# Two-layer hybrid backbone on one core: filter unit ends spread over the next unit, spectra stored by GpSimd's queue, weights prepared with loads ahead, an early pool lower in SBUF

## The chip, the core and the metric

The kernel runs on one core of a Trainium2 chip. The metric is the device time of one execution in microseconds, lower is better. TensorE (PE) multiplies matrices, VectorE (DVE), ScalarE (ACT) and GpSimd (POOL) work on tiles, SyncE (SP) issues most of the transfers; each engine takes its instructions strictly in the order in which the program wrote them.

## The reference, cut to what matters

Layer 0 mixes a pooling branch with grouped-query attention, layer 1 mixes a Hyena branch (two long convolutions by FFT) with a Fourier branch. The change touches work that belongs to layer 1 but needs none of its inputs, and is done under the attention of layer 0: the Hyena filters with their spectra, and the weights in split form.

```python
def one_block(qblk):                       # layer 0, attention
    s = jnp.einsum('bqhgd,bkhd->bhgqk', qblk, k) * scale
    p = jax.nn.softmax(s, axis=-1).astype(v.dtype)
    return jnp.einsum('bhgqk,bkhd->bqhgd', p, v)
...
def hyena_filters(L, w1, b1, w2, b2, w3, freq):
    ...
    h = (hdn @ w3.astype(f32)).reshape(L, HY_ORDER, 2, HY_WIDTH)
    decay = jnp.exp(-t * jnp.abs(deltas))
    h = h * decay[:, None, None, :]
    h = h / (jnp.sum(jnp.abs(h), axis=(0, 2), keepdims=True) + EPS)
...
def fft_long_conv(z, kfull):
    zf = jnp.fft.rfft(z, n=2 * L, axis=1)
    kf = jnp.fft.rfft(kfull, n=2 * L, axis=0)
```

2048 tokens, 6 query heads of 128, 2304 keys (256 of context), and 12 filter units of 128 channels (6 groups of channels, 2 orders).

## The kernel before, in words

Five stages follow each other: the projections of layer 0 (to about 599 us), attention (to 1766), the output projection of layer 0 (to 2075), the projections of layer 1 (to 2808), and the convolutions' end, the Fourier branch and the output.

**Attention and what lies in it.** Attention walks 96 blocks (6 heads, 8 query tiles, 2 halves). The order within a block is a string `BLOCK[..]` of letters: `S` scores, `M` the maximum, `E` exponentials, `T` transposes, `V` products with the values, `D` and `N` the division. Two letters put other work between them. `F` (and `f` in every eighth pair of blocks) is a fill: it takes one step of the generator `filters`, and when that has ended, of `wout`. `p` takes one step of the generator `weights`. Strings 0 and 1 serve even and odd blocks until `filters` has ended, strings 2 and 3 after that. At that end `for _ in prep: pass` writes out what is left of `weights` in one go, before the next letter of the block; then its pool `aside` is closed.

**The filters.** 12 units of 8 groups. A group is a fill with the product `hacc` of the hidden features (`hd`) with `w3`, a DVE product `ht` with the decay (`dec`), a reduction `rd` of the absolute values, and a fill with the products `fa`, which ACT copies into the spectrum `fX`. At a unit's end the eight `rd` are reduced to `rs`, summed over the partitions on TensorE (`smacc`), and turned into a scale `sc_n` and the pair `sd`, from which the last `fa` comes: 18 fills for a unit. Then GpSimd transforms `fX` by an FFT of 46 instructions. `some()`, called in every fill, hands these to GpSimd's order: it lets `FFT_US` of the instructions' listed cost pass for each call. The finished spectrum (2 MB) is stored by SP, `FFT_LATE` fills after the last FFT instruction.

**The weights.** 23 items of the first kind (a block of the layer-1 input weights) and 32 of the second (output weights, multiplied by a gate). An item loads `wraw`, (second kind) multiplies it by `wgb` on GpSimd, casts it on ACT to the high half of `wodd`, subtracts on GpSimd to get the low half, and stores `wodd` through SP. An item of the second kind spreads over six `p`: load, multiply, nothing, cast, subtract, store. After the items come two products `fnp` with the DFT matrix.

Of the kernel before, what the change touches and what calls it, by code (L numbers as in the profile page):

```python
# [248 lines left out]
def tile_net(ctx, tc, i, k, out, keep=None):  # L249
# [233 lines left out]
    LASTE, LASTR, GATE2, FOLD1, HALF, SUM0, SUM1, ADDF, FEW, LASTW, IN_C, FFT_US, FFT_LATE, FILTER_X, HL, DR, DE, EW0, EW1, SPLIT, SUMMED, QSEL, CV0, CV1, CV2, CV3, COL, NW0, NW1, FIRST_Z, MORE, X0_SQ, X0_STEP, TRAIL, C_EARLY, A_TURN, A_SLOW, A_AHEAD, A_W, A_PACE, LAG0, FOLD, WAIT, AHEAD, LAG, APART, LOW, W_LOAD, W_HIGH, W_LOW, ADDED, SLOW = 0, 0.5, 5, 6, 1.5, 0.2, 1.5, 3, 9, 3.5, 25, 4.4, 4, 2, 3, 4, 4, 8.0, 2.5, 15, 0.5, 1, 14, 12, 8, 15, 5, 24, 0, 20.0, 8, [7, 7, 11, 11], (0, 0, 0, 0, 2, 2, 2, 2), 11, 1, 2.5, 0.25, 3.5, 4, 1.05, 7, 2, 6.0, 2.5, 5, 5, 2, 6, 6, 4, 8, 1.02  # L483
# [16 lines left out]
    with ExitStack() as st, tc.manual_schedule(engines=EVERY):  # L500
        sp = pool(st, "a_sb", 2)
# [5 lines left out]
        def pair(name):  # L507
            x2 = sp.tile([P, KD, 256], F32, tag="wmb", name=name)
# [47 lines left out]
        with ExitStack() as s2:  # L556
# [24 lines left out]
            hd2 = sp.tile([P, 4, 2, HD], F32, tag="sq", name="hd2", bufs=1).rearrange("p t h d -> p (t h d)")  # L581
# [208 lines left out]
        def heads(raw, ss, nt, tb, nm, dst, col0):  # L790
# [9 lines left out]
            else:  # L800
                rt = ropes[tb, nm]
                sq = sp.tile([P, 4, 2, HD], F32, tag="sq", name="sq", bufs=1)
# [30 lines left out]
        def modulation():  # L833
# [5 lines left out]
            def load(blk):  # L839
                n, c0 = (0, 2048 + 256 * blk) if blk < 4 else (1, 256 * (blk - 4))  # L840
                wms[blk] = sp.tile([P, KD, 256], F32, tag="wmb", name="wmb")
# [44 lines left out]
        def mixer():  # L886
# [3 lines left out]
            for m in range(2):  # L890
# [7 lines left out]
                uf = sp.tile([P, N2, P], F32, tag="wmb", name="uf")  # L898
                sy.dma_start(uf, src)
                sg = sp.tile([P, N2, P], F32, tag="wmb", name="psg")  # L900
                sy.dma_start(sg, sg0[m].rearrange("p (a b) -> p a b", a=N2))
                yield 0.0, 12.0
                for c in range(2):
                    c0 = 64 * c
                    us = sp.tile([P, 2, 32, 64], F32, tag="xt", name="us", bufs=1)
# [217 lines left out]
    def filters(st, psum, tag, after):  # L1123
# [8 lines left out]
        late, ops = [], []  # L1132
        got, room = {}, [0.0]

        def some():

            due[0] += 1
            room[0] = min(room[0] + FFT_US, FFT_US)
            while ops and room[0] > 0:
                us, op = ops.pop(0)  # L1140
                room[0] -= us
                if callable(op):
                    op()
                else:
                    late.append((due[0] + FFT_LATE, op))
            if late and late[0][0] <= due[0]:
                sy.dma_start(*late.pop(0)[1])

        due = [0]
# [9 lines left out]
        def fetch_w3(u):  # L1159
# [6 lines left out]
            skr = sp.tile([1, P], F32, tag="skr", name="skr", bufs=2)  # L1166
            sy.dma_start(skr, i["hy_skip"][0, o : o + 1, jl])
            got[u] = raw, skr

        def split_w3(u):  # L1170
            raw, skr = got[u]
# [3 lines left out]
            got[u] = w, skr  # L1175

        fetch(0, 0)
        fetch_w3(0)
        yield
# [3 lines left out]
        for u in range(2 * NCH):  # L1183
            j, o = u // 2, u % 2
            w3, skr = got.pop(u)
            rd = sp.tile([P, 8, P], F32, tag="rd", name="rd")
            X = sp.tile([P, 2, N2, P], F32, tag="X", name="fX", bufs=FILTER_X)
            for grp, (n, m) in enumerate(PAIRS):
                last = grp == 7
                if (u, grp) != (2 * NCH - 1, 7):  # L1190
                    fetch(u + grp // 7, (grp + 1) % 8)
                dec, hd = got.pop((u, grp))
                ht = sp.tile([P, 2, 2, P], F32, tag="ht", name="ht", bufs=2)
                acc = psum.tile([P, 2, 2, P], F32, tag=tag, name="hacc")
                for q in range(2):
                    for x in range(2):
                        w = w3[:, x, ::-1] if q else w3[:, x]
                        pe.matmul(acc[:, q], hd[:, q, :], w, start=x == 0, stop=x == 1)
                after(1, lambda: v.tensor_mul(ht, acc, dec.unsqueeze(2).to_broadcast([P, 2, 2, P])))
                yield  # L1200
                some()
                v.tensor_reduce(out=rd[:, grp, :], in_=ht.rearrange("p a d b -> p b (a d)"), axis=AX.X, op=ALU.add,
                                apply_absolute_value=True)
                if u + 1 < 2 * NCH and grp in (3, 6):
                    (fetch_w3 if grp == 3 else split_w3)(u + 1)
                if last:
                    rs = sp.tile([P, P], F32, tag="rs", name="rs")
                    v.tensor_reduce(out=rs, in_=rd.rearrange("p a b -> p b a"), axis=AX.X, op=ALU.add)
                    yield
                    sm = psum.tile([P, 512], F32, tag=tag, name="smacc")  # L1210
                    pe.matmul(sm[:, 0:1], rs, ones[:, 0:1], start=True, stop=True)
                    pe.matmul(sm[0:1, P : 2 * P], ones[:, 0:1], rs, start=True, stop=True)
                    sd = sp.tile([P, 2, 2, P], F32, tag="ht", name="sd", bufs=2)

                    def scaled():
                        idx = o * NCH + j
                        v.tensor_scalar(out=sc_n[:, idx : idx + 1], in0=sm[:, 0:1], scalar1=EPS, scalar2=None, op0=ALU.add)
                        rw = sp.tile([1, P], F32, tag="rw", name="rw")
                        v.scalar_tensor_tensor(out=rw, in0=sm[0:1, P : 2 * P], scalar=EPS, in1=skr, op0=ALU.add, op1=ALU.mult)
                        v.reciprocal(sc_n[:, idx : idx + 1], sc_n[:, idx : idx + 1])  # L1220
                        v.tensor_add(ht[0:1, 0, 0, :], ht[0:1, 0, 0, :], rw)
                        v.memset(ht[0:1, 0, 1, :], 0.0)
                        v.tensor_add(sd[:, 0], ht[:, :, 0], ht[:, :, 1])
                        v.tensor_sub(sd[:, 1], ht[:, :, 0], ht[:, :, 1])


                    after(2, scaled)
                    yield
                fa = psum.tile([P, 2, 2, P], F32, tag=tag, name="fa")
                for r in range(2):  # L1230
                    for q, b in enumerate((n, m)):
                        if last:
                            pe.matmul(fa[:, r, q], dft[:, b, r, :], sd[:, r, q], start=True, stop=True)
                        else:
                            pe.matmul(fa[:, r], dft[:, b, r, :], ht[:, q], start=q == 0, stop=q == 1)
# [1190 lines left out]
```

## Time and profile before

| what | us |
|---|---|
| median of 3 runs | 3177.69 (3174.78 to 3182.2) |
| the profiled execution | 3177.3 |
| its span | 3175.5 |
| TensorE busy in it | 2937.0 (92%) |
| attention stage, first to last | about 603 to 1766 |

The profiled execution is 0.4 us below the median and 1.8 us above its own span. Times inside the trace count from the start of the span. TensorE is busy nearly all the time, so what it waits for in a stage is what that stage could lose; its busy time also stretches where the granted clock is below 1.

### The profile page before, as it was taken

What the parts mean: (1) busy time and instruction counts of PE and PEld (TensorE: products, weight loads), DVE (VectorE), ACT (ScalarE), POOL (GpSimd) and SP (SyncE); (2) the same over time, 40 slices, a digit from 0 to 9 for tenths busy, and PEclk for the clock granted to TensorE, in tenths of its full rate; (3) what the DMA queues carried; (4) which work ended last, traced back from release to release, by engine and by line L of the source; (5) the groups of instructions that cost most, each with busy time, mean ns of one, the idle gap of its engine ahead of it and who ended that gap; (6) DMA issues with size and microseconds to landing.
All of it is one profiled execution on the core that took longest, in us unless ns stands there. A gap on an engine that the chain in (4) does not pass through costs nothing. (4 is left out here: it accounts for less than half of the span.)

```text
span 3175.5 us, 46860 instructions
## 1 busy us (share of the span) xinstructions
PE 2937.0 (92%) x16969; PEld 2520.1 (79%) x16969; DVE 2149.7 (68%) x3981; ACT 1323.7 (42%) x3048; POOL 1132.7 (36%) x1091
## 2 busy tenths in 40 slices
PE   7999999799999999999986999999989999988799
PEld 4898888688888888888875778777878777874587
DVE  4676327477777777777764343377879797978556
ACT  4444445365655555556554232322323222231223
POOL 3122122117877778788871344001010010100110
PEclk9999999899999999999998999999999999989899
DMA  6466335534443343333325577689899989976875
GB/s 219 147 206 206 107 135 172 168 100 129 128 134 115 112 148 105 112 118 112 104 77 214 183 268 252 242 268 292 275 307 277 289 275 302 278 235 184 218 205 175
DMA packets 346707, 602.74 MB, mean 190 GB/s; under 512 B 41894, under 2 KB 216168, under 8 KB 336490
## 3 DMA queue, kind: packets, MB, share of 16 engines
q1 hardware_dynamic: 321178, 516.37, 47.9%
q0 software_dynamic: 25152, 83.10, 11.1%
q8 instruction: 134, 2.20, 0.3%
q14 instruction: 99, 0.81, 0.1%
q10 hardware_dynamic: 144, 0.26, 0.0%
HBM read 376.80 MB, written 187.18 MB: 178 GB/s over the span
## 5 line engine op out<-in xcount | busy, mean ns | idle before, releaser
L312 DVE TENSOR_TENSOR pl<-pt,ph 128x512 fp32r<-128x512 f32 (+1 forms) x480 | 299.0, 633 | 171.8 <-ACT ph L309 165.0
L155 DVE TENSOR_TENSOR gB<-gB 128x256 f32<-128x256 f32 (+3 forms) x442 | 351.6, 845 | 47.6 <-ACT gB L1933 43.8
L1338 ACT ACTIVATE pb<-S,mx 128x512 f32<-128x512 f32 (+1 forms) x480 | 310.1, 657 | 161.2 <-DVE mx L1330 161.1
L315 PE MATMUL dacc<-dh,dw 128*128 128x512 f32 x768 | 311.4, 406 | 45.8 <-DMA dh<-h1T 44.5
L309 ACT CAST ph<-pt 128x512 fp32r<-128x512 f32 (+1 forms) x480 | 257.6, 556 | 220.0 <-PE pt L1349 218.8
L1327 DVE TENSOR_REDUCE mx<-S 128x1 f32<-128x512 f32 (+1 forms) x480 | 279.7, 629 | 54.4 <-PE S L317 40.5
L316 PE MATMUL dacc<-dh,dw 128*128 128x512 f32 x768 | 304.1, 396 | 0.0
L317 PE MATMUL dacc<-dh,dw 128*128 128x512 f32 x768 | 303.7, 395 | 0.0
L312 POOL TENSOR_TENSOR wl<-raw,wh 128x256 fp32r<-128x256 f32 x160 | 136.3, 884 | 374.9 <-ACT wh L309 329.7
L1349 PE MATMUL pt<-ident,pb 128*128 128x128 f32 x1728 | 252.2, 276 | 9.5 <-ACT pb L1338 8.4
L1361 PE MATMUL o<-ph,vh 128*128 128x256 f32 x864 | 232.4, 300 | 0.3
L155 POOL TENSOR_TENSOR fT<-fX 128x1024 f32<-128x1024 f32 (+2 forms) x120 | 191.3, 1623 | 115.9 <-ACT fX L1236 114.6
L1349 PEld LDWEIGHTS pt<-ident,pb 128*128 128x128 f32 x1728 | 201.7, 142 | 31.6 <-ACT pb L1338 16.4
L1362 PE MATMUL o<-ph,vl 128*128 128x256 f32 x864 | 218.4, 284 | 2.6 <-DMA vl<-vl 2.6
L155 POOL TENSOR_TENSOR fX<-fT 128x256 f32<-128x256 f32 (+2 forms) x168 | 219.2, 1329 | 2.5
L315 PE MATMUL S<-kh,qh 128*128 128x512 f32 (+1 forms) x480 | 200.0, 417 | 21.3 <-DVE pl L312 10.5
L315 PEld LDWEIGHTS dacc<-dh,dw 128*128 128x128 f32 x768 | 147.0, 191 | 84.7 <-DMA dh<-h1T 42.1
L315 PE MATMUL acc<-wh,hh 128*128 128x256 f32 x672 | 198.1, 295 | 6.6 <-DVE hh L311 3.4
L317 PE MATMUL acc<-wh,hl 128*128 128x256 f32 x672 | 193.9, 289 | 1.0 <-DVE hl L312 0.9
L316 PE MATMUL acc<-wl,hh 128*128 128x256 f32 x672 | 193.7, 288 | 0.9 <-POOL wl L312 0.8
L316 PE MATMUL S<-kl,qh 128*128 128x512 f32 (+1 forms) x480 | 181.9, 379 | 0.7 <-DMA kl<-kT1l 0.7
L317 PE MATMUL S<-kh,ql 128*128 128x512 f32 (+1 forms) x480 | 181.9, 379 | 0.0
(476 smaller groups left out, 7406.3 us busy)
## 6 DMA issues: line engine op xcount, KB each, us to landing
dh<-h1T SPq DMA_DIRECT2D x172, 512.0 KB
spec<-fX SPq DMA_DIRECT2D x12, 2048.0 KB
dw<-wi SPq DMA_DIRECT2D x48, 512.0 KB
gK<-spec SPq DMA_DIRECT2D x48, 512.0 KB
raw<-in_ev_w_in_dram SPq DMA_DIRECT2D x160, 128.0 KB
u<-dev SPq DMA_DIRECT2D x70, 256.0 KB
cu<-u POOLq DMA_DIRECT2D x17, 1024.0 KB, 8.0
wmb<-in_w_mod_dram SPq DMA_DIRECT2D x16, 1024.0 KB
```

Source lines behind the costliest of these rows:

```text
L155: put(out, lambda: v.tensor_tensor(out=out, in0=in0, in1=in1, op=op))
L309: s.copy(hi, src)
L312: lo_eng.tensor_sub(lo, src, hi.bitcast(F32))
L315: pe.matmul(acc, ah, bh, start=first, stop=False)
L316: pe.matmul(acc, ah, bl, start=False, stop=False)
L317: pe.matmul(acc, al, bh, start=False, stop=last)
L1327: v.tensor_reduce(out=B["mx"][:, c : c + 1], in_=S[:, :n], axis=AX.X, op=ALU.max)
L1338: s.activation(B["pb"][:, c * 512 : c * 512 + n], B["S"][c][:, :n], AF.Exp, bias=B["mx"][:, 5:6], accum_out=B["sm"][:, c : c + 1])
L1349: pe.transpose(pt[:, t, :], B["pb"][:, (4 * c + t) * P : (4 * c + t + 1) * P], ident)
L1361: pe.matmul(gr["o"], vh[:, a, :], ph[:, t, :], start=a == 0, stop=False)
L1362: pe.matmul(gr["o"], vl[:, a, :], ph[:, t, :], start=False, stop=False)
```

## The change

Five parts. (1) `BLOCK[0]` gets one more `p` at its end: seven steps of `weights` in a pair of blocks instead of six. (2) `FFT_US` goes from 4.4 to 5.0; `FFT_LATE` goes, and the spectrum's store is the FFT's last entry, issued from GpSimd's queue. (3) A unit's end moves between the first pieces of the next unit: `hacc` of group 0 of the next unit, then `smacc`, then the next unit's first `rd` and `fa`, then the last `fa` of the unit that ends: 17 fills a unit instead of 18. The final reduction is made in two parts (five `rd` after group 4, then four at the end), `ht` gets three buffers, the pair `sd` is made one tick after the scale, and the skip row is loaded at group 6. The load for group 1 of unit 0 is issued before the 2 MB matrix `fdft`. (4) In `weights` the next load is issued right after the subtraction, and an item of the second kind takes five `p`: multiply (with the store of the item before), nothing, cast, subtract and load, nothing. (5) The tiles `wmb`, `xt` and `sq` of the projection stage move to a pool of their own, `a_x`, opened first.

```diff
@@ BLOCK
-    "T0 p S0 S1 F S2 S3 S4 M T1 f p F D V3 V4 E1 N E3 T2 E0 T3 p E4 E2 F T4 Z",
+    "T0 p S0 S1 F S2 S3 S4 M T1 f p F D V3 V4 E1 N E3 T2 E0 T3 p E4 E2 F T4 p Z",
@@ constants
-    ... IN_C, FFT_US, FFT_LATE, FILTER_X ... = ... 25, 4.4, 4, 2 ...
+    ... IN_C, FFT_US, FILTER_X ... = ... 25, 5.0, 2 ...
@@ early pool
+        xp = pool(st, "a_x", 2)
         sp = pool(st, "a_sb", 2)
...
-                xt = sp.tile([P, 4, D], F32, tag="xt", name="xt", bufs=1)
+                xt = xp.tile([P, 4, D], F32, tag="xt", name="xt", bufs=1)
@@ filters
         fetch(0, 0)
         fetch_w3(0)
+        fetch(0, 1)
         yield
         sy.dma_start(dft, k["fdft"])
...
+        def sums(st_, grp):
+            u, rd = st_["u"], st_["rd"]
+            v.tensor_reduce(out=rd[:, grp - 3 * (grp > 4), :], in_=st_[grp].rearrange("p a d b -> p b (a d)"), axis=AX.X, op=ALU.add,
+                            apply_absolute_value=True)
...
+            if grp in (4, 7):
+                lo, hi, to = (0, 5, 5) if grp == 4 else (2, 6, 0)
+                v.tensor_reduce(out=rd[:, to, :], in_=rd[:, lo:hi].rearrange("p a b -> p b a"), axis=AX.X, op=ALU.add)
...
+            after(2, scaled)
+            after(3, both)
...
+        def transform(st_):
+            u, X = st_["u"], st_["X"]
+            T = sp.tile([P, 2, N2, P], F32, tag="T", name="fT")
+            ops.extend([(0.04 + 2.05 * us, fn) for fn, us in fft16(g, X, T, False, g, True)])
+            ops.append((0.6, lambda: g.dma_start(specd[u // 2][u % 2], X)))
...
+        for u in range(2 * NCH + 1):
...
+                features(st_, 0)
+            yield
+            some()
+            if last:
+                norm(last)
+                yield
+            if st_:
+                sums(st_, 0)
+                spectrum(st_, 0)
+            if last or st_:
+                yield
+                some()
+            if last:
+                spectrum(last, 7)
+                yield
+                transform(last)
+                some()
@@ weights
+            nxt = load(*items[0])
+            yield
+            for x, (n, kk, half) in enumerate(items):
+                raw = nxt
+                if half is not None:
+                    g.tensor_mul(raw, raw, gate[0])
+                    yield
+                    yield
                 w = wp.tile([P, 2, 512], F32R, tag="w", name="wodd")
                 s.copy(w[:, 0], raw)
                 yield
                 g.tensor_sub(w[:, 1], raw, w[:, 0].bitcast(F32))
+                if x + 1 < len(items):
+                    nxt = load(*items[x + 1])
                 yield
                 yield
-                mv(dst, w)
+                mv(..., w)
```

SP's order at the head of the attention stage, the last stores of the projections' rotated queries (`qT4h` to `qT5l`) and the loads of attention's first queries (`qh`, `ql`), with the semaphores that they wait for; before:

```order
L261 DMA qT4h<-qhi 128x512 [waits DMAHW4_49,Activation_49]
L261 DMA qT4l<-qlo 128x512 [waits DMAHW5_49,DVE_49]
L261 DMA qT5h<-qhi 128x512 [waits DMAHW6_49,Activation_49]
L261 DMA qT5l<-qlo 128x512 [waits DMAHW7_49,DVE_49]
L261 DMA qh<-qT0h 128x256 [waits DMAHW4_49,DMAHW3_49,DMAHW5_49,DMAHW2_49,DMAHW6_49,DMAHW1_49,DMAHW7_49,DMAHW0_49,Activation_49]
L261 DMA ql<-qT0l 128x256
```

and with the change (the names of semaphores are the program's):

```order
L261 DMA qT4h<-qhi 128x512 [waits DMAHW4_49,Activation_49]
L261 DMA qT4l<-qlo 128x512 [waits DMAHW5_49,DVE_49]
L261 DMA qT5h<-qhi 128x512 [waits DMAHW6_49,Activation_49]
L261 DMA qT5l<-qlo 128x512 [waits DMAHW7_49,DVE_49]
L261 DMA qh<-qT0h 128x256 [waits DMAHW4_49,DMAHW3_49,DMAHW5_49,DMAHW2_49,DMAHW6_49,DMAHW1_49,DMAHW7_49,DMAHW0_49,Activation_49]
L261 DMA ql<-qT0l 128x256
```

Nothing moved there: the first query load waits for the same semaphores, and the counts that it waits for are the same too.

DVE's order at the end of the first filter unit, before (`rs` is the final reduction, `sc_n` to `sd` what follows `smacc`, `pl` and `mx` are attention's):

```order
L1330 TENSOR_REDUCE mx<-mx 128x1
L1202 TENSOR_REDUCE rd<-ht 128x128
L1208 TENSOR_REDUCE rs<-rd 128x128
L312 TENSOR_TENSOR pl<-pt,ph 128x4x128 x2
L1217 TENSOR_SCALAR sc_n<-smacc 128x1
L1219 SCALAR_TENSOR_TENSOR rw<-smacc,skr 1x128
L1220 RECIPROCAL sc_n<-sc_n 128x1
L1221 TENSOR_TENSOR ht<-ht,rw 1x128
L1222 MEMSET ht 1x128
L1223 TENSOR_TENSOR sd<-ht 128x256
L1224 TENSOR_TENSOR sd<-ht 128x256
```

and with the change, at the same place:

```order
L1375 TENSOR_REDUCE mx<-mx 128x1
L1198 TENSOR_REDUCE rd<-ht 128x128
L1206 TENSOR_REDUCE rd<-rd 128x128
L1193 TENSOR_TENSOR ht<-hacc,dec 128x512
L312 TENSOR_TENSOR pl<-pt,ph 128x4x128 x2
L1218 TENSOR_SCALAR sc_n<-smacc 128x1
L1220 SCALAR_TENSOR_TENSOR rw<-smacc,skr 1x128
L1221 RECIPROCAL sc_n<-sc_n 128x1
L1222 TENSOR_TENSOR ht<-ht,rw 1x128
L1223 MEMSET ht 1x128
L312 TENSOR_TENSOR pl<-pt,ph 128x2x128
L1227 TENSOR_TENSOR sd<-ht 128x256
```

The last reduction is followed by the next unit's first product `ht`, and `sd` comes one piece of attention later.

GpSimd's order where one FFT ends and the next begins, while items of the second kind are prepared (`wraw<-wraw,wgb` is the multiply before a cast, `wodd` the subtraction after it, `fT` and `fX` the FFT); before:

```order
L155 TENSOR_TENSOR fX<-fT 128x2x2x128
L1435 TENSOR_TENSOR wraw<-wraw,wgb 128x512
L155 TENSOR_TENSOR fX<-fT 128x2x2x128
L1415 TENSOR_TENSOR wodd<-wraw,wodd 128x512
L1435 TENSOR_TENSOR wraw<-wraw,wgb 128x512
L155 TENSOR_TENSOR fT<-fX 128x1024 x2
L1415 TENSOR_TENSOR wodd<-wraw,wodd 128x512
L155 TENSOR_TENSOR fT<-fX 128x1024 x2
L155 TENSOR_TENSOR fX<-fT 128x2x512 x4
L1435 TENSOR_TENSOR wraw<-wraw,wgb 128x512
```

and with the change:

```order
L155 TENSOR_TENSOR fX<-fT 128x2x2x128 x2
L1478 TENSOR_TENSOR wraw<-wraw,wgb 128x512
L1250 DMA spec_0_153<-fX 128x4096
L1484 TENSOR_TENSOR wodd<-wraw,wodd 128x512
L1478 TENSOR_TENSOR wraw<-wraw,wgb 128x512
L1484 TENSOR_TENSOR wodd<-wraw,wodd 128x512
L155 TENSOR_TENSOR fT<-fX 128x1024 x4
L155 TENSOR_TENSOR fX<-fT 128x2x512
L1478 TENSOR_TENSOR wraw<-wraw,wgb 128x512
L155 TENSOR_TENSOR fX<-fT 128x2x512 x2
```

The whole of an FFT now stands before one more item's end, and the spectrum's store stands in GpSimd's own order, right after the FFT.

Counted in blocks of attention, in TensorE's order: before, the last `fa` stands at block 85, the weights' last cast and the two `fnp` at block 91, and the strings 2 and 3 serve the last 5 blocks. With the change the two `fnp` stand at blocks 75 and 76, the last `fa` at block 81, and the strings 2 and 3 serve the last 11 blocks. From the output projection on, all orders are the same.

## Rows read from the trace of the kernel before

**Rows 1.** The page: span and TensorE.

```profile
span 3175.5 us, 46860 instructions
PE 2937.0 (92%) x16969; PEld 2520.1 (79%) x16969; DVE 2149.7 (68%) x3981; ACT 1323.7 (42%) x3048; POOL 1132.7 (36%) x1091
```

**Rows 2.** Windows of the attention stage: length, busy time by engine, granted clock, DMA.

```profile
core 0: us, PE busy (x) PEld busy (x) DVE busy (x) ACT busy (x) POOL busy (x), PEclk, DMA share, GB/s
640.00:1600.00 960.00, 927.31 (x6264) 844.59 (x6262) 743.45 (x1445) 563.45 (x1472) 700.50 (x581) 0.99 0.37 117
1600.00:1680.00 80.00, 68.23 (x444) 58.96 (x442) 47.11 (x102) 43.28 (x116) 63.72 (x53) 0.96 0.30 107
1680.00:1715.00 35.00, 12.51 (x59) 10.45 (x60) 4.29 (x9) 5.05 (x12) 5.04 (x4) 0.66 0.37 120
1715.00:1766.00 51.00, 45.83 (x329) 40.71 (x327) 33.90 (x70) 31.94 (x82) 0.00 (x1) 1.00 0.48 183
```

**Rows 3.** TensorE's waits from 590 to 1770: total, times, longest.

```profile
PE fnp L1450 <- DMA wraw<-cst_dftd_dram: 19.1, 1, 19.1
PE smacc L1211 <- DVE rs L1208: 13.5, 11, 2.1
...
PE S L315 <- DMA kl<-kT0l: 8.0, 1, 8.0
PE hacc L1198 <- DMA hd<-hdd: 6.0, 1, 6.0
PE fa L1235 <- DVE ht L1199: 4.7, 4, 1.6
PE fa L1233 <- DVE sd L1223: 4.4, 3, 1.7
```

**Rows 4.** Timeline of SP around the head of attention: start, duration, instruction.

```profile
595.28 0.41 SPq L261 DMA_DIRECT2D qT5l<-qlo  x1
602.01 0.32 SPq L261 DMA_DIRECT2D qh<-qT0h  x1
629.23 0.38 SPq L261 DMA_DIRECT2D hd<-hdd  x1
```

**Rows 5.** Timeline of the ends of units 0 and 2, DVE and TensorE.

```profile
694.94 0.38 PE L1211 MATMUL smacc<-ones,rs 128*128 128x1 f32 x2 [2.10 <-DVE rs L1208]
...
855.24 1.89 DVE L1208 TENSOR_REDUCE rs<-rd 128x128 f32<-128x1024 f32 x1
857.18 0.38 PE L1211 MATMUL smacc<-ones,rs 128*128 128x1 f32 x2 [2.09 <-DVE rs L1208]
```

**Rows 6.** Timeline of TensorE where the rest of the weights is written out.

```profile
1698.43 3.75 PE L1450 MATMUL fnp<-wraw 128*128 128x256 f32 x8 [19.15 <-DMA wraw<-cst_dftd_dram]
```

**Rows 7.** GpSimd's weight work by line, 640 to 1700: count, busy, mean ns, idle before.

```profile
L1415 POOL TENSOR_TENSOR wodd<-wraw,wodd 128x512 fp32r<-128x512 f32 x54 | 69.7, 1290 | 131.0 <-ACT wodd L1413 131.0
L1435 POOL TENSOR_TENSOR wraw<-wraw,wgb 128x512 f32<-128x512 f32 x32 | 41.8, 1307 | 32.9 <-DMA wraw<-in_od_w_out_dram 22.2 <-DMA wraw<-in_ev_w_out_dram 10.7
```

**Rows 8.** Timeline of GpSimd and ACT: a multiply and the cast behind it; an FFT's start.

```profile
1154.98 1.30 POOL L1435 TENSOR_TENSOR wraw<-wraw,wgb 128x512 f32<-128x512 f32 x1
1156.98 0.64 ACT L1413 CAST wodd<-wraw 128x512 fp32r<-128x512 f32 x1
1194.36 9.40 POOL L155 TENSOR_TENSOR fT<-fX 128x1024 f32<-128x1024 f32 x4 [7.86 <-ACT fX L1236]
```

**Rows 9.** Timeline of ACT and TensorE where a multiply came too late, and ACT's waits.

```profile
1631.53 0.62 ACT L1413 CAST wodd<-wraw 128x512 fp32r<-128x512 f32 x1 [4.66 <-POOL wraw L1435]
1633.41 0.50 PE L315 MATMUL S<-kh,qh 128*128 128x512 f32 x1 [4.34 <-DVE pl L312]
...
ACT pb L1338 <- DVE mx L1330: 161.1, 48, 4.4
...
ACT wodd L1413 <- POOL wraw L1435: 20.8, 5, 7.0
```

**Rows 10.** A store issued from GpSimd's queue in the next stage.

```profile
1773.27 0.58 POOL L261 DMA_DIRECT2D wi<-iw  x1 [0.30 <-POOL iw L1791]
```

More of the change, by code (lines that the diff above doesn't have):

```diff
@@ L1131, in filters @@
         dft = fc.tile([P, N2, 2, P], F32, name="fdft")
-        late, ops = [], []
+        ops = []
         got, room = {}, [0.0]
         def some():
-            due[0] += 1
             room[0] = min(room[0] + FFT_US, FFT_US)
@@ L1141, in some @@
                 room[0] -= us
[L1142 to L1149, printed above, removed]
+                op()
         def fetch(u, grp):
@@ L1182, in filters, with features @@
         yield
[L1183 to L1199, printed above, removed]
+        def features(st_, grp):
+            u = st_["u"]
+            if (u, grp) not in ((0, 0), (2 * NCH - 1, 7)):
+                fetch(u + grp // 7, (grp + 1) % 8)
+            dec, hd = got.pop((u, grp))
+            w3 = st_["w3"]
+            ht = st_[grp] = sp.tile([P, 2, 2, P], F32, tag="ht", name="ht", bufs=3)
+            acc = psum.tile([P, 2, 2, P], F32, tag=tag, name="hacc")
+            for q in range(2):
+                for x in range(2):
+                    w = w3[:, x, ::-1] if q else w3[:, x]
+                    pe.matmul(acc[:, q], hd[:, q, :], w, start=x == 0, stop=x == 1)
+            after(1, lambda: v.tensor_mul(ht, acc, dec.unsqueeze(2).to_broadcast([P, 2, 2, P])))
@@ new lines, in spectrum @@
+        def spectrum(st_, grp):
+            if "X" not in st_:
+                st_["X"] = sp.tile([P, 2, N2, P], F32, tag="X", name="fX", bufs=FILTER_X)
+            X, (n, m) = st_["X"], PAIRS[grp]
+            fa = psum.tile([P, 2, 2, P], F32, tag=tag, name="fa")
+            for r in range(2):
+                for q, b in enumerate((n, m)):
+                    if grp == 7:
+                        pe.matmul(fa[:, r, q], dft[:, b, r, :], st_["sd"][:, r, q], start=True, stop=True)
+                    else:
+                        pe.matmul(fa[:, r], dft[:, b, r, :], st_[grp][:, q], start=q == 0, stop=q == 1)
+            after(3, lambda: s.copy(X[:, :, n : m + 1 : m - n, :], fa))
@@ L1200, in filters @@
                 yield
                 some()
[L1202 to L1208, printed above, removed]
-                    yield
[L1210 to L1235, printed above, removed]
-                after(3, lambda: s.copy(X[:, :, n : m + 1 : m - n, :], fa))
@@ L1237, in filters @@
-                yield
-                if last:
-                    T = sp.tile([P, 2, N2, P], F32, tag="T", name="fT")
-                    ops += [(0.04 + 2.05 * us, fn) for fn, us in fft16(g, X, T, False, g, True)]
-                    ops.append((0.0, (specd[j][o], X)))
-                some()
-        while ops or late:
+            if last:
[3 more added lines that the diff above has]
+                some()
+            if st_ is None:
+                break
@@ L1244, in filters @@
+            for grp in range(1, 8):
+                features(st_, grp)
+                yield
+                some()
+                sums(st_, grp)
+                if grp < 7:
+                    spectrum(st_, grp)
+                    yield
+                    some()
+            last = st_
+        while ops:
             some()
@@ L1409, in raws, with load @@
                 return wp.tile([P, 512], F32, tag="raw", name="wraw", bufs=2)
-            def parts(raw, dst):
+            items = [(n // KD, n % KD, None) for n in range(48 - IN_C)]
+            items += [(n, kk, half) for n in range(2) for half in range(2) for kk in range(KD)]
+            gate = [None]
+            def load(n, kk, half):
+                raw = raws()
+                if half is None:
+                    for h in range(2):
+                        load_columns(raw[:, h * 256 : h * 256 + 256].rearrange("p (a b) -> p a b", a=2), n, kk, h)
+                    return raw
+                hl = slice(half * 512, half * 512 + 512)
+                if kk == 0:
+                    gate[0] = wp.tile([P, 512], F32, tag="gate", name="wgb")
+                    sy.dma_start(gate[0], gated[n].rearrange("(o a) b -> o (a b)", o=1)[:, hl].to_broadcast([P, 512]))
+                sy.dma_start(raw, (i["ev_w_out"][0], i["od_w_out"][0])[n][kk * P : (kk + 1) * P, hl])
+                return raw
+            nxt = load(*items[0])
[6 more added lines that the diff above has]
+                    yield
                 w = wp.tile([P, 2, 512], F32R, tag="w", name="wodd")
```

76 lines of the change are left out of this document (44 added, 32 removed).

## The prediction

> **What bounds the kernel now.** I read the page first: TensorE is busy 2937.0 of 3175.5 us [rows 1], so only what it waits for, or does at a low clock, can be had. The engines' orders are the same before attention and from the output projection on, so everything is decided between 600 and 1766 us. The windows say where [rows 2]. From 640 to 1600 TensorE idles 32.7 of 960 us (3.4%) at a clock of 0.99: little to gain. From 1600 to 1680 it idles 11.8 of 80, from 1680 to 1715 22.5 of 35 at a clock of 0.66, and in the last 51 us, in five blocks without any other work, 5.2 us, which is 1.03 a block. Then the list of waits gives the names [rows 3]: in the drain of the weights one of 19.15 us [rows 6], at units' ends 13.5 us in 11 for `smacc` and 4.4 in 3 for `sd`, at the head 8.0 for the first keys and 6.0 for `hd`. The reader should see that the largest item is a serial tail in which one item after another goes load, multiply, cast, subtract, store with nothing beside it, since the filters have ended before the weights.
>
> **The change, part by part.** The sum is made against the profiled execution's own 3177.3 us.
>
> *Early pool.* The first query load issues at 602.01, 6.3 us after SP's store before it ended its issue (595.28 + 0.41) [rows 4]. In the order it waits for the same semaphores at the same counts as before, so I put 0. If the freed place let it go at once, 6.3 us of the 8.0 us wait for the first keys [rows 3] would go: the other bound is -6.3.
>
> *First loads.* `hd` of group 1 issues at 629.23 [rows 4], behind the 2 MB matrix and the values, and TensorE waits 6.0 us for it [rows 3]. It now issues ahead of them. Group 2's load is the next that is late: it stands where group 1's stood, but its product comes two fills later. I take -5 (0 to -6).
>
> *Unit ends.* What is to be had is 13.5 + 4.4 us, and of the 4.7 us of `fa` waiting for `ht` [rows 3] some. `sd` now has another fill between it and its `fa`: its 4.4 go, and new `ht` waits may take 1 or 2 back. `smacc` is different. Before, DVE makes `rs` in 1.89 us and TensorE stands 2.09 us for it [rows 5]. In the new order the last reduction reads four slots, not eight (half of 1.89, an estimate of 0.95), but the next unit's `ht` product follows on DVE, and `smacc` still stands one fill after the last `ht`, with one product `hacc` between. So each wait shrinks by about an `rs` half, 0.9 us, and only where there is one: -5 of the 13.5. I take -9 in all; the bounds are -3 (only `sd`) and -18 (all).
>
> *Tail and drain.* Before, 1600 to 1715 holds 11.8 + 22.5 = 34.3 us of idle, and 68.23 x 0.04 + 12.51 x 0.34 = 7.0 us of low clock [rows 2]: 41.3 us. In the changed order the weights end at block 76, inside the filter phase (seven `p` a pair and five steps an item in place of six and six), so the drain is empty and the pool closes at once. What takes its place: the strings without fills serve 11 blocks, not 5, and lose 1.03 us each [rows 2], which is 6; and the blocks up to there wait 3.4% like the rest, 1 to 2. So 41.3 - 8 = 33 (-25 to -40, the lower bound if the two `fnp` wait for their loads inside the filters, the upper if the extra blocks lose nothing).
>
> *GpSimd's lag.* This is the cost. Two unit ends lie at 694.94 and 857.18 [rows 5], so a unit is 81.1 us, a fill 81.1/18 = 4.51 us, and a pair of blocks, 3.5 to a unit, 23.2 us. GpSimd is busy 700.5 + 63.7 + 5.0 us in attention [rows 2], of which 69.7 + 41.8 are the weights [rows 7]: 54.8 us for each of 12 FFTs. The listed cost of an FFT is 55.0 by the code's own formula. At 4.4 a fill it is laid into 12.5 fills, 56.4 us; with the weights of 2.4 items at 2.6 us [rows 7], GpSimd has 61 us of work there, ends 4.7 us late, and the cast, two `p` (7.7 us) behind its multiply, does not notice: the tightest one that I found follows its multiply by 0.7 us [rows 8]. At 5.0 the FFT is laid into 11 fills, 49.6 us; with an item in every 5/7 of a pair, 16.6 us, three items are in it, 7.8 us: 62.6 us of work, 13.0 late, while the cast is now only 2/7 of a pair, 6.6 us, behind its multiply. It is 6.4 us short, once in each of the seven units in which items of the second kind are made (32 x 16.6 = 531 us): 45 us of ACT waiting in front of `wodd`. Behind that cast on ACT stand the exponentials `pb` and the casts `ph`, and TensorE waits for these. In the tail a wait of 4.66 us on ACT became one of 4.34 on TensorE [rows 9], 0.93 of it; by that row it costs 42. Elsewhere ACT idles in each such place anyway: 161.1 us in 48 waits for `mx`, 3.4 each [rows 9], which leaves 3.0 of the 6.4, or 21. The idle time of ACT is spread over the filled stretch where these waits lie, so I am nearer to the second and take +24 (0, if GpSimd's idle 7.86 us before an FFT [rows 8] takes it up as well, to +50).
>
> *Spectra by GpSimd.* Twelve issues; the nearest row is a store from the same queue at 0.58 us [rows 10], together 7 us on GpSimd, mostly inside its idle time between units. SP loses twelve waits for FFTs. I put 0 (to +4).
>
> A rule speaks against this one. The Trainium skill (SBUF — State Buffer, section "SBUF: two separate sides") says that GpSimd writes the descriptors of a transfer issued from its queue, and that it cannot while VectorE runs an instruction that holds both ports: about 620 ns alone and 3100 ns beside such an instruction, by that page. The row of 0.58 us stands where VectorE was working too, and agrees with the lower figure. By the higher one twelve issues would hold GpSimd for some 37 us, an estimate from the page, and more multiplies would come late (rival E).
>
> Sum: -5 - 9 - 33 + 24 = -23, and 3177.3 - 23 = 3154. The median of the runs lies 0.4 us above the profiled execution, so the forecast for it is 3155.
>
> **The rivals.**
> (A) GpSimd's lag costs nothing: ACT's idle time and GpSimd's gaps between FFTs swallow it, and the time is 3177.3 - 47 = 3130. For it: at the tightest place before, 0.7 us were left and nothing was lost [rows 8]. Against it: 6.4 us is twice ACT's idle stretch.
> (B) The lag costs all and more, and the kernel becomes slower. A late cast makes the subtraction late, SP stands before the store that waits for it, and behind that store stand the next `dec` and `hd`; each late unit then costs a wait like the 6.0 us of `hd` [rows 3] on top of its 6.4: 7 x 12.4 x 0.93 = 81 at worst. The point from which it decides is 47 us, 6.7 a unit. At 55 to 60 the time is about 3188. For it: SP is one queue for stores and loads. Against it: the loads of a group are issued a fill ahead (4.5 us), and the next raw load no longer waits for the store.
> (C) The drain's gain is smaller, as the filters are slowed by seven steps of weights a pair: -15 in place of -33, 3172. TensorE's own work does not grow by it, so little speaks for it.
> (D) The early pool does free the keys: 3148, inside the range.
> (E) An issue from GpSimd's queue takes longer beside VectorE than 0.58 us [rows 10]. If it waits out one of VectorE's long instructions, 1.89 us [rows 5], ahead of the multiply that stands behind it, each of the seven units loses 1.9 x 0.93 more: +12, 3167. The page named above would have it so.
>
> **How the numbers follow.** The forecast as worked, 3140 to 3172: 0.44. A: 0.24. B: 0.13. C: 0.10. D: 0.05. E: 0.04. A difference of 0.2% (6.4 us) is about what a measurement of this kernel can tell from none. The range goes from A with the whole of the units' ends, 3122, to B's beginning, 3187. Faster, below 3171, gets A, D, E and the forecast without its upper edge: 0.72. Same, 3171 to 3184, gets that edge, and C: 0.14. Slower is B and a little of C's: 0.14.
>
> **What would show it.** Right: no `fnp` wait of 19 us and no stretch at a clock of 0.66 near 1700; the filled part ending about 1630 and 11 blocks behind it; `smacc` waiting still, about 1 us each; ACT's waits for `wraw` at 30 to 50 us, in two to three places of each unit from the fourth to the tenth; the first query load still at 602. Wrong: ACT waits for `wraw` below 15 us (then A), TensorE waiting for `hd` several times or for `S` and `pt` by more than 50 us (then B), or a tail that has merely moved.

## The result, and the profile after

The changed kernel is slower: 3190.51 us median (3180.18 to 3198.7, 17 runs) against 3174.78 (3164.88 to 3182.2, 17 runs), a ratio of 1.0055 [1.0042, 1.0068]. The forecast was 3155 with a range to 3187, and slower had a chance of 0.14.

The page after, its span and engines:

```profile
span 3194.4 us, 46876 instructions
PE 2941.9 (92%) x16969; PEld 2521.2 (79%) x16969; DVE 2148.2 (67%) x3993; ACT 1325.4 (41%) x3048; POOL 1142.1 (36%) x1103
```

The profiled execution took 3196.16. Windows of the attention stage after (columns as in [rows 2]):

```profile
640.00:1600.00 960.00, 893.54 (x5938) 809.23 (x5937) 703.26 (x1369) 534.28 (x1385) 722.11 (x603) 0.98 0.38 123
1600.00:1680.00 80.00, 75.40 (x525) 67.20 (x525) 57.41 (x126) 49.57 (x136) 55.84 (x47) 1.00 0.11 35
1687.00:1700.00 13.00, 1.20 (x9) 0.99 (x7) 2.69 (x7) 2.32 (x6) 0.00 (x0) 0.62 0.97 396
```

From 640 to 1600 TensorE idles 66.5 us where it idled 32.7 [rows 2]: 34 us lost in the stretch that was to gain. The stretch after 1600 is better than before, as forecast, but there is a hole at 1687. TensorE's waits after:

```profile
PE pt L1394 <- ACT pb L1383: 26.3, 27, 5.5
PE S L315 <- DVE pl L312: 16.0, 14, 4.1
PE hacc L1192 <- DMA hd<-hdd: 13.0, 5, 4.1
PE S L315 <- DMA qh<-qT5h: 11.8, 1, 11.8
PE S L315 <- DMA kl<-kT0l: 8.1, 1, 8.1
PE hacc L1192 <- ACT fX L1244: 7.3, 5, 3.5
PE smacc L1213 <- DVE ht L1193: 5.8, 5, 1.7
```

Two of these waits were smaller before:

```profile
PE S L315 <- DVE pl L312: 10.5, 4, 4.3
PE pt L1349 <- ACT pb L1338: 8.4, 22, 0.8
```

The wait of 19.1 for `fnp` [rows 6] is gone and `smacc` fell from 13.5 [rows 3] to 5.8. The waits behind ACT grew: `pt` waits for ACT's exponentials, and `S` for VectorE's `pl`, which waits for ACT's cast `ph`. `hd` was one wait of 6.0 [rows 3] and is 13.0 in five places; one of 11.8 for a query is new. ACT and SP tell why; ACT's waits after:

```profile
ACT wodd L1482 <- POOL wraw L1478: 38.7, 12, 7.6
ACT wodd L1482 <- DMA wi<-wodd: 12.2, 2, 10.7
ACT wodd L1482 <- DMA we<-wodd: 10.5, 2, 8.1
ACT wodd L1482 <- DMA wo<-wodd: 10.0, 2, 7.6
ACT wodd L1482 <- DMA dec<-cst_decay_dram: 9.5, 1, 9.5
...
ACT wodd L1482 <- issue: 4.9, 1, 4.9
```

and one of SP's:

```profile
SPq L261 <- DMA spec<-fX: 35.1, 1, 35.1
```

ACT stands 38.7 us in front of `wodd` for late multiplies (20.8 before, 20.3 of it in the tail, behind 1600 us) and, which the prediction did not have, 47 us more for the place of `wodd` itself: it has one buffer, and the next cast waits until the store of the item before has landed, which waits for GpSimd's subtraction (the last two rows, put down to another transfer and to nothing, I count with these: a store of `wodd` had been issued 6.9 and 3.1 us before those casts). Four of these eight casts, 26.6 us, belong to items of the first kind, and four, 20.5 us, to items of the second. The chain in one place, an item of the first kind, GpSimd, SP, ACT, TensorE and VectorE after:

```profile
842.60 1.26 POOL L1484 TENSOR_TENSOR wodd<-wraw,wodd 128x512 fp32r<-128x512 f32 x1
843.89 0.32 SPq L261 DMA_DIRECT2D wi<-wodd  x1
846.98 0.62 ACT L1482 CAST wodd<-wraw 128x512 fp32r<-128x512 f32 x1 [10.75 <-DMA wi<-wodd]
848.34 1.54 PE L1394 MATMUL pt<-ident,pb 128*128 128x128 f32 x6 [5.47 <-ACT pb L1383]
849.46 0.69 DVE L312 TENSOR_TENSOR pl<-pt,ph 128x512 fp32r<-128x512 f32 x1 [9.51 <-ACT ph L309]
```

The subtraction stands in the middle of an FFT; SP's store, ACT's next cast and TensorE's transposes follow it one by one, and 10.75 us of ACT became 5.47 us of TensorE. Behind SP's store stood `dec` and `hd`.

### The profile page after: what moved, and what is told of

Read it like the earlier page. It is cut to its first block, busy times and chain, and to the rows that moved or that the text cites. A ratio compares the mean times of both kernels' runs of the same rounds, so it can differ in the third digit from the quotient of the medians.

```text
span 3194.4 us, 46876 instructions
## 1 busy us (share of the span) xinstructions
PE 2941.9 (92%) x16969; PEld 2521.2 (79%) x16969; DVE 2148.2 (67%) x3993; ACT 1325.4 (41%) x3048; POOL 1142.1 (36%) x1103
## 5 line engine op out<-in xcount | busy, mean ns | idle before, releaser
L315 PE MATMUL dacc<-dh,dw 128*128 128x512 f32 x768 | 312.3, 407 | 45.8 <-DMA dh<-h1T 44.5
```

Source lines behind the costliest of these rows:

```text
L315: pe.matmul(acc, ah, bh, start=first, stop=False)
```

## The experiments

Executions with the same order of instructions before attention reached its first query load between 593.6 and 603.7 us, so spans are compared only over attention: from SP's first `qh` load to GpSimd's first `iw` load, which waits for attention's last block. Before that is 1766.0 - 602.0 = 1164.0 us, after 1787.4 - 603.7 = 1183.7. "Filters" is from the same `qh` to the last unit's `smacc`. Both columns are one execution each: up to that `smacc` e4 has the same order as the changed kernel, and e23 the same as e18, and these pairs differ by 4.5 and 3.4 us. The ratios stand on 4 to 17 runs each. Each is to the kernel before as measured beside that run: a median of 3169.07 to 3171.94 us in the rows of the experiments, 3174.78 in the changed kernel's own.

| run | ratio to before | 95% | filters | attention |
|---|---|---|---|---|
| before | 1 | | 994.6 | 1164.0 |
| changed kernel | 1.0055 | 1.0042, 1.0068 | 1005.8 | 1183.7 |
| e1_fft44 | 0.9898 | 0.9879, 0.9916 | 963.6 | 1136.9 |
| e3_split | 1.0080 | 1.0059, 1.0100 | 1012.7 | 1190.3 |
| e4_late_wout | 1.0025 | 1.0011, 1.0038 | 1010.3 | 1176.7 |
| e5_weights_only | 0.9880 | 0.9861, 0.9899 | 1007.3 | 1133.3 |
| e6_ends_only | 1.0257 | 1.0244, 1.0270 | 1018.8 | 1246.7 |
| e9_fft44_late | 0.9906 | 0.9887, 0.9925 | 961.3 | 1130.7 |
| e10_before_fft50 | 1.0122 | 1.0106, 1.0139 | 1020.8 | 1206.2 |
| e13_mul_dve | 1.0023 | 1.0010, 1.0036 | 998.2 | 1175.2 |
| e14_weights_fft40 | 0.9894 | 0.9875, 0.9913 | 1005.9 | 1134.8 |
| e16_all_fft40_late | 0.9851 | 0.9831, 0.9870 | 954.8 | 1122.9 |
| e17_fft44_spec_sp | 0.9845 | 0.9826, 0.9865 | 956.4 | 1119.5 |
| e18_weights_spec_pool | 0.9912 | 0.9894, 0.9930 | 1011.5 | 1142.7 |
| e8_fft50_spec_sp | 0.9992 | 0.9977, 1.0006 | 998.2 | 1162.3 |
| e20_fft40_spec_sp | 0.9909 | 0.9892, 0.9926 | 971.6 | 1135.8 |
| e21_pool_only | 0.9996 | 0.9984, 1.0008 | 993.1 | 1162.8 |
| e23_weights_spec_pool_late | 0.9900 | 0.9885, 0.9915 | 1008.1 | 1132.7 |

(The filters' end lies four blocks earlier in the kernels with the new ends, so that column is to be compared only among kernels with the same ends.)

**Theory L**, GpSimd's lag: the FFT's larger share puts too much of it ahead of each multiply and subtraction, ACT stands at the casts, and TensorE behind ACT. **Theory U**: the new ends of the units cost it. **Theory S**: SP's wait for the last spectrum costs it.

### The share alone, from both sides

e1, the changed kernel:

```diff
-    ... 3.5, 25, 5.0, 2, ...
+    ... 3.5, 25, 4.4, 2, ...
```

> The changed kernel with the FFT's share set back from 5.0 to 4.4 a fill, nothing else. Theory L (GpSimd falls behind, its multiplies and subtractions come late, ACT stands at the casts and TensorE behind ACT): ACT's waits in front of wodd, 86 us in the changed kernel (38.7 for multiplies, 47 for stores of the item before), fall to 20 to 45 us, TensorE's idle time from 640 to 1600 from 66 to 40 to 50 us, and the time is 3160 to 3175. Theory U (the interleaved ends of the units cost the time, by products waiting for fX and for hd): 3184 to 3196, no change. Theory S (SP's wait of 35 us for the last spectrum) changes nothing here or makes it later by one or two fills.

3140.07 us: faster than L's own numbers, and U falls. ACT's waits for `wodd` in e1 (first load left out):

```profile
ACT wodd L1482 <- POOL wraw L1478: 11.6, 4, 6.0
ACT wodd L1482 <- DMA wi<-wodd: 9.6, 3, 5.4
ACT wodd L1482 <- DMA wo<-wodd: 5.1, 1, 5.1
...
ACT wodd L1482 <- DMA dec<-cst_decay_dram: 3.1, 1, 3.1
```

86 us became 30, and attention 46.8 us shorter, 42.2 of it within the filters. e10 is the mirror, the kernel before with the share at 5.0:

```diff
-    ... 3.5, 25, 4.4, 4, ...
+    ... 3.5, 25, 5.0, 4, ...
```

> The kernel before with the FFT's share at 5.0 a fill and nothing else: six steps a pair, six steps an item. Theory L as in the prediction: 11 fills of 4.5 us for 54.8 us of FFT and 2.1 items at 2.6 us, 10.7 us late at the end, the cast 7.7 us behind its multiply: 3 us short in each of eight or nine units, 10 to 25 us slower, 3180 to 3195. If 5.0 only costs together with the seventh step and the five-step items: 3165 to 3177.

3206.48 us, attention 42.2 us longer, beyond L's number and far from the other. 26.2 of it lie within the filters and 16.0 behind them, in the drain of the weights, where `fnp` waits 23.6 us instead of 19.1 and `S` for `pl` 17.5 instead of 10.5. ACT's waits for multiplies in e10:

```profile
ACT wodd L1413 <- POOL wraw L1435: 49.4, 13, 7.7
```

So the share costs by itself, and neither the seventh step nor the five-step items are needed for it.

### Which wait behind the lag

e3 gives each half of `wodd` its own tile and stores the high half early:

```diff
-                w = wp.tile([P, 2, 512], F32R, tag="w", name="wodd")
-                s.copy(w[:, 0], raw)
+                hi = wp.tile([P, 512], F32R, tag="wh", name="whigh")
+                s.copy(hi, raw)
                 yield
-                g.tensor_sub(w[:, 1], raw, w[:, 0].bitcast(F32))
+                mv(dst[:, 0, :], hi)
+                w = wp.tile([P, 512], F32R, tag="wl", name="wlow")
+                g.tensor_sub(w, raw, hi.bitcast(F32))
```

> The changed kernel with wodd in two tiles of half the size, the high half stored right after the cast, the low half where the whole was stored. ACT's next cast then no longer waits for the store that stands behind GpSimd's late subtraction. Theory L: of ACT's 86 us in front of wodd the 47 us for stores fall below 15, and the time is 3165 to 3180. If only the late multiplies count (39 us, which stay), 3184 to 3196.

3196.52 us: no gain. The waits for stores did go from ACT (47 us became 12.0), to SP. TensorE's largest wait in e3:

```profile
PE hacc L1192 <- DMA hd<-hdd: 31.6, 7, 10.7
```

13.0 in five places became 31.6 in seven: SP now stands before two stores an item, with `hd` behind them. The run does not say what the waits for stores cost, only that they can be moved. e13 moves the multiply to VectorE:

```diff
-                    g.tensor_mul(raw, raw, gate[0])
+                    v.tensor_mul(raw, raw, gate[0])
```

> The changed kernel, FFT at 5.0, with the multiply by the gate on VectorE in place of GpSimd: the casts no longer wait behind GpSimd's FFT for it, the subtractions and so the stores still do. If the multiplies are what costs (39 us of ACT's waits): 3155 to 3172. If the stores of one late subtraction hold the next cast (47 us of ACT's waits, which stay or grow), 3178 to 3190. VectorE gets 32 more instructions of about 0.7 us, 22 us spread over seven units, beside 74% of busy time.

3177.3 us, in neither span: the 38.7 us for multiplies are gone from ACT's waits, and attention is 8.5 us shorter. Late multiplies were the smaller part of the lag's cost, or VectorE's added work took some of it back; the run cannot part these.

### The single parts

e5, the kernel before with parts 1 and 4 alone (`weights` as in the diff ahead, `BLOCK[0]` with its fourth `p`).

> The kernel before with the new preparation of the weights alone (loads ahead, five steps an item, seven steps a pair of blocks), FFT at 4.4, units' ends and spectra as before. The prediction's term for tail and drain (33 us) shows by itself: 3140 to 3155 against the kernel before at 3175, less what GpSimd's lag costs at this pace; theory L with 2.2 us of slack gone: 3150 to 3165. If the drain's time is given back elsewhere: 3170 to 3180.

3134.03 us, attention 30.7 us shorter: the filters, which now hold all of the weights and both `fnp`, take 12.7 us longer, and what comes behind them 43.4 less. It is the tail's term, net of what the lag costs at this pace. e14 is e5 with the share at 4.0.

> The kernel before with the new preparation of the weights (as in the run with the weights alone), and the FFT's share at 4.0 a fill. Theory L: the FFT is laid into 13.8 fills, GpSimd falls behind no more than at the old pace, and of ACT's 25 us in front of wodd for multiplies and stores half go: 3124 to 3133 beside the kernel before at 3169. If the rest of ACT's waits comes from places that the share does not touch, 3133 to 3138.

3138.62 us, no gain. ACT's waits behind GpSimd fell from 24 (16.7 and 6.9) to about 5, and attention did not get shorter: in this kernel that much lag seems to be covered, though a wait of ACT for the spectrum's store (5.4 us in 2) came up in its place. ACT's waits in e14:

```profile
ACT wodd L1437 <- POOL wraw L1433: 3.6, 2, 3.1
ACT wodd L1437 <- DMA wi<-wodd: 1.7, 1, 1.7
```

e6, the changed kernel with parts 1, 2 and 4 undone (the spectra go to SP again, four fills after the FFT's last entry):

```diff
-            ops.append((0.6, lambda: g.dma_start(specd[u // 2][u % 2], X)))
+            ops.append((0.0, (specd[u // 2][u % 2], X)))
```

> The changed kernel with parts 1, 2 and 4 undone: six steps a pair, FFT at 4.4, spectra by SP four fills after the FFT, the weights as before. What is left is the units' ends between the next unit's pieces, the early load and the early pool. By the prediction's terms (9 for the ends, 5 for the first load) 3155 to 3165 beside a kernel before at 3170. Since the changed kernel at 4.4 came out 6 us slower than the weights alone, the rival says that the ends gain nothing: 3165 to 3178. The drain of the weights then still stands, 17 fills a unit ending the filters earlier, so that more of it is left: that alone would make it 5 to 15 slower.

3250.59 us, far outside both. The drain grew (its `fnp` waits 34.1 us), but most is something else. ACT's copies into `fX` in e6, three of the eight rows over 1 us:

```profile
1041.24 0.59 ACT L1252 COPY fX<-fa 128x512 f32<-128x512 f32 x1 [19.87 <-DMA spec<-fX]
...
1303.71 0.59 ACT L1252 COPY fX<-fa 128x512 f32<-128x512 f32 x1 [14.74 <-DMA spec<-fX]
...
1548.93 0.59 ACT L1252 COPY fX<-fa 128x512 f32<-128x512 f32 x1 [13.33 <-DMA spec<-fX]
```

There are two `fX`. With the new ends a unit's first `fa` comes before the unit ahead of it has its last, so the spectrum of two units back must be out sooner than with the old ends; four fills' delay is too late. The parts hang together: the new ends need an early store. This run is no measure of the ends' gain; e17 is.

e21, the early pool alone (the `xp` lines of the diff, in the kernel before).

> The kernel before with the early pool alone. The prediction's term: no difference, ratio 0.998 to 1.002, the first query load at the same distance of 6 to 7 us behind the last store of the projections. If the freed place lets the first keys go: 6 us faster.

0.9996 [0.9984, 1.0008]: nothing, as forecast; `qh` issues 6.7 us behind `qT5l` (598.42 against 591.71), as before.

### The spectra's route and the end of the filters

e4, the changed kernel, and e9, the same at 4.4:

```diff
         def wout():
+            for _ in range(8):
+                yield
```

> The changed kernel with the loads of layer 0's output weights begun eight fills (four blocks) later, so that they no longer stand in SP's queue before the last spectrum has landed. Theory S: SP's wait of 35.1 us and TensorE's wait of 11.8 us for qh go, and the low clock behind it: 3174 to 3182. If SP's wait costs nothing because another wait takes its place (the same loads late at the end of attention): 3186 to 3196.

> The changed kernel with the FFT at 4.4 a fill and the output weights' loads begun eight fills later. If the wait for qh (6.7 us at 4.4) goes as it did at 5.0 (a gain of about 10 there): 3128 to 3136. If it was covered at 4.4, where the FFT ends nearer to the filters' end: 3138 to 3144.

e4: 3176.72 us, the wait for `qh` gone and attention 7.0 us shorter: theory S holds, for a part. e9: 0.9906 beside e1's 0.9898; attention is 6.2 us shorter by one execution, 3.9 of it behind the filters, but the times show no difference. The delay has a place of its own in e9: from 1676 to 1696 TensorE waits again, 3.07 us at most, for a `pl` that stands behind ACT, and ACT there waits 3.13 us before the cast of the next stage's input `y`.

e17, the changed kernel at 4.4 with the store given back to SP, two fills after the FFT, and e8, the same at 5.0:

```diff
-            ops.append((0.6, lambda: g.dma_start(specd[u // 2][u % 2], X)))
+            ops.append((0.0, (specd[u // 2][u % 2], X)))
...
-        while ops:
+        while ops or late:
...
+                if callable(op):
+                    op()
+                else:
+                    late.append((due[0] + 2, op))
+            if late and late[0][0] <= due[0]:
+                sy.dma_start(*late.pop(0)[1])
```

> The changed kernel with the FFT at 4.4 a fill (which came out at 3140), and the spectra stored by SP two fills after the FFT's last entry instead of by GpSimd right behind it. If the new ends depend on that store (the third unit's fX needs the place of the first one's a unit's end earlier than before): ACT waits for the spectrum's store before fX, several us a unit, and the time is 3170 to 3230. If the way of the store is of no account, 3135 to 3145.

> The changed kernel, FFT at 5.0, with the spectra stored by SP two fills after the FFT's last entry. If the route adds to the share of 5.0 as it did at 4.4 (17 us): 3165 to 3178 beside a kernel before at 3171. If SP, standing before the store until the late FFT ends, holds up hd and dec: 3190 to 3215.

Both expectations on e17 fell: 3121.85 us, by the ratios 17 us faster than e1. e8: 3163.84, 21 us of attention shorter than the changed kernel. Of e17's 17.4 us of attention, 7.2 lie within the filters and 10.2 behind them; of e8's 21.4, 7.6 and 13.8. Behind the filters the traces point to theory S. Windows of e1 around its wait for `qh`, and SP's wait for the last spectrum in the same run:

```profile
1640.00:1660.00 20.00, 15.83 (x86) 13.67 (x87) 8.41 (x17) 6.34 (x17) 0.00 (x0) 0.75 1.01 406
1660.00:1680.00 20.00, 17.80 (x121) 16.56 (x120) 14.41 (x29) 12.93 (x32) 0.00 (x0) 0.91 0.30 81
```

and

```profile
SPq L261 <- DMA spec<-fX: 35.0, 1, 35.0
```

SP stands 35 us before the output weights' loads, which take the spectra's place in SBUF; a query load stands behind them, TensorE idles 6.7 us for it, and the clock is 0.75 and 0.91 in the two windows around that. With SP's store the filters' generator ends only when that store stands in SP's order, two fills later. SP's rows in e17, and the same two windows:

```profile
SPq L1148 <- POOL fX L155: 53.9, 9, 28.1
SPq L261 <- DMA spec<-fX: 2.5, 1, 2.5
```

```profile
1640.00:1660.00 20.00, 18.92 (x134) 16.99 (x133) 14.01 (x33) 13.39 (x38) 0.00 (x0) 1.00 0.90 331
1660.00:1680.00 20.00, 17.82 (x124) 15.61 (x123) 14.82 (x31) 13.53 (x34) 0.00 (x0) 1.00 0.09 27
```

SP's standing is not gone: it waits 28.1 us for the last FFT, before the store. But a query load now stands between that store (1621.68) and the first load of an output weight (1628.61); TensorE has no wait for `qh`, and the clock stays at 1.00. Whether this order gives the gain or the two fills' delay alone is not shown: e9, which takes the wait away by a delay, has only 3.9 of the 10.2 us.

The 7 us within the filters I could not place; ACT's wait for a spectrum's store before `fX` is 16.1 us in e1 and 8.8 in e17, but of the changed kernel and e8, 7.6 us apart, neither has such a wait, so the cause stays open.

Between e17 and e8 only the share differs: attention 42.8 us, 41.8 of them within the filters. ACT's waits for `wodd` are 29.5 us in e17 and 74.0 in e8, of which the rows are these and one of 5.1 put down to nothing:

```profile
ACT wodd L1490 <- POOL wraw L1486: 37.4, 11, 7.5
ACT wodd L1490 <- DMA wi<-wodd: 16.4, 3, 10.7
ACT wodd L1490 <- DMA wo<-wodd: 10.1, 2, 7.7
ACT wodd L1490 <- DMA we<-wodd: 5.0, 2, 2.5
```

e18 is e5 with the spectra stored by GpSimd, e23 the same with the output weights eight fills later.

> The kernel before with the new preparation of the weights and the spectra stored by GpSimd right after the FFT, ends of the units as before, FFT at 4.4. By the row of 0.58 us an issue and with SP freed of its waits for the FFT: 3130 to 3137, no difference to the weights alone (3134). If an issue from GpSimd's queue takes several times that beside VectorE, as the Trainium skill (SBUF — State Buffer, section "SBUF: two separate sides") has it for instructions that hold both ports: later multiplies, 3140 to 3150.

> The kernel before with the new weights, spectra by GpSimd, and the output weights' loads eight fills later. If GpSimd's store cost 8 us through the end of the stage, where SP's loads wait for the last spectrum: back to 0.987 to 0.989 of the kernel before, as with the weights alone. If the issue itself on GpSimd costs: 0.990 to 0.993, as without the delay.

e18: 0.9912, e23: 0.9900, e5: 0.9880. GpSimd's store costs here too, some 10 us (9.4 of attention; the 4.2 of them within the filters are no more than the scatter above), and the intervals do not tell how much of it the delay gives back. In e23 attention is 10.0 us shorter than in e18, but right behind it TensorE waits 8.3 us for the next stage's `y`, whose loads the delay has moved too. The time of e18 lies in the span of its second case, but not by that case's mechanism, for the issue itself is short on GpSimd's queue, in e18:

```profile
L1241 POOL DMA_DIRECT2D spec<-fX x12: 621/621/787, 757.1 to 1671.0; - x12
```

0.62 us in the median and 0.79 at most, so the multiple named by the Trainium skill (SBUF — State Buffer, section "SBUF: two separate sides") is not what these twelve issues show. VectorE worked beside eleven of them; whether in instructions that hold both ports was not looked at.

e16 and e20 set the share to 4.0, one with GpSimd's store and late output weights, one with SP's store.

> The changed kernel with the FFT at 4.0 a fill and the output weights' loads eight fills later. With 17 fills a unit the FFT takes 13.8 of them, so the spectrum is out two fills before the next but one unit needs its place. Theory L: 3124 to 3134. If the ends between the next unit's pieces need the spectrum earlier than this (fX waiting for the spectrum's store), 3145 to 3180.

> The changed kernel with the FFT at 4.0 a fill and the spectra stored by SP two fills after the FFT's last entry. If ACT's waits for late multiplies (10.6 us at 4.4) go and nothing takes their place: 3112 to 3120. If fX waits for the spectrum's store instead, as the FFT now takes 13.8 of 17 fills and the store two more: 3122 to 3160.

e16: 3123.02 us, 1 us below its first span. Against e9, its neighbour at 4.4, attention is 7.8 us shorter (6.5 within the filters), and the intervals of the ratios lie apart. e20: 3138.78, its second case: `fX` waits for the spectrum's store, ACT's row in e20:

```profile
ACT fX L1252 <- DMA spec<-fX: 36.4, 9, 7.6
```

So share and route are one setting: an FFT laid out longer needs its store sooner. The best versions are e17, 0.9845 [0.9826, 0.9865], and e16, 0.9851 [0.9831, 0.9870], 1.5% faster than the kernel before and 2% faster than the change.

## Why the prediction was wrong, point by point

The steps add up along four kernels. From before to e5 -30.7 us of attention, from e5 to e17 -13.8, from e17 to e1 +17.4, from e1 to the changed kernel +46.8: +19.7 in all, where the forecast had -23. Of the 43 us between them 23 are the lag's, 17 the spectra's and 2 the tail's. What a step costs depends on what stands already: the spectra's move costs 17.4 at this place, 21.4 with the share at 5.0 and 9.4 on e5.

- **Tail and drain**: forecast -33, measured -30.7 in e5. Right, in mechanism and size: in the changed kernel both `fnp` run inside the filters, at 1541 and 1564, with no wait of 19 us.
- **Unit ends and first loads**: forecast -9 and -5, measured -13.8 together (with the early pool's nothing). Right in sum; the step also holds the store's delay of two fills in place of four, and the two terms were not measured apart. `smacc` still waits, 9.6 us in 8 in e17 against 13.5 in 11. `sd`'s 4.4 are gone, but a wait of `fa` for the skip row `rw`, 3.3 us in 3, took most of their place. The first load's gain is smaller than said: the wait of 6.0 for `hd` is replaced by one of 3.8 (3.5 in the changed kernel) for the matrix `fdft`, now behind that load. Group 2's load was not the next one late.
- **Early pool**: forecast 0, measured 0.9996.
- **Spectra by GpSimd**: forecast 0 (to +4), measured +17.4. The price of an issue was right at 0.62 us, though not by the row that was read for it: around 1773.27 VectorE stands idle, from 1766.6 to 1776.3, so that row [rows 10] was no sign of an issue beside a working VectorE; eleven of e18's twelve are, and rival E falls with them. The step that failed is "SP loses twelve waits for FFTs". SP's waits before, from 600 to 1850, have none in front of these twelve stores: the delay of four fills had already kept them free. It also kept the filters' generator open until the last spectrum was on its way, and with it the output weights' loads out of SP's queue. So nothing was lost, and one wait of 35 us came. How the 17.4 us divide stays partly open: 7.2 have no cause shown, and of the 10.2 behind the filters e9 gave back 3.9.
- **GpSimd's lag**: forecast +24 (0 to +50), measured +46.8 between e1 and the changed kernel, 42.2 of it within the filters; +42.2 of attention in e10. The mechanism was right, the term was mis-sized by nearly half. Two steps of it failed. "Once in each of the seven units in which items of the second kind are made" counted only casts that wait for their multiply (45 us forecast, 38.7 measured). It left out that every cast also waits for the one `wodd` buffer, behind store and subtraction: 47 of the 86 us, 26.6 at items of the first kind, which have no multiply, and 20.5 at items of the second. And I took the price of 0.5 from ACT's idle stretches instead of the 0.93 of the only row in which this wait had been seen [rows 9]; measured within the filters were 42.2 us for 55 us of waits (86 - 30), 0.76, and with SP's store, from e17 to e8, 41.8 us for 44.5 (74.0 - 29.5), 0.94. The cover that I counted on is small where there is any: e14 took some 20 us of ACT's waits away and gained nothing, but with the new ends, from e9 to e16, 18 us less (30.7 to 13.0) gained 7.8.

Rival B named the direction, and its mechanism, `hd` behind SP's store, is there with 13.0 us in five places, but it is the smaller part: 7 us more than before, where `pt` and `S` behind ACT have 42.3 against 18.9, 23 more. The range ended 3.5 us short.

## What to carry to other kernels

A helper engine's share of work is priced by what stands behind its late instruction on each in-order queue, buffers included: here a subtraction on GpSimd held SP's store, the store held the one buffer, the buffer held ACT, and ACT held TensorE. Where a wait has been seen once in a trace, its row's price belongs in the forecast beside any argument about cover. Before a wait is counted as saved, look for it in the trace. When a delay is taken out, ask what else it kept apart, above all loads that reuse the delayed transfer's place and the loads queued behind them.

## What was not expected of the hardware

With the same instruction order, the first 600 us took between 593.6 and 603.7 us from execution to execution, so differences below about 10 us between two profiled spans say nothing unless they are taken over a stretch, and over the filters, too, two executions of one order differed by up to 4.5 us. After a stall with TensorE idle for most of 13 us (1687 to 1700) its granted clock was 0.62 over these, and 0.96 over the next 50.
